# Half-row matmuls of a mixer block issued as alternating pairs, with new settings of the kernel's own scheduler

## The chip, the core and the metric

The kernel runs on one core of a Trainium2 chip. The metric is the device time of one execution in microseconds (us), lower is better. All times here are of this one core; "the profile" is one profiled execution of the kernel before, with its trace.

## What is computed

A causal decoder trunk of two layers over 256 tokens of width 1024, all in fp32. Cut to what matters here:

```python
for l in range(DEPTH):                                   # 2 layers
    h = modulate(rms_norm(x, norm_mix[l]), sh1, sc1)
    p = h @ w_in[l]                                      # one wide projection
    q, k = apply_rope(...), apply_rope(...)              # 8 heads of 64
    y_att  = dilated_mixture_attention(q, k, v)          # scores q.k over a head's 64 channels
    y_rwkv = rwkv7_time_mix(p[..., i0:i1], ...)          # decay: tanh(xw) @ w_up, rate: xa @ a_up, inner width 64
    y_gmlp = chunked_spatial_gating(p[..., i1:i2], ...)
    merged = sum(sigmoid(gate_i) * (y_i @ w_branch[l][i]))
    x = x + gt1 * (merged @ w_out[l])
    h = modulate(rms_norm(x, norm_ffn[l]), sh2, sc2)
    x = x + gt2 * conv_gated_ffn(h, w_up, conv, w_down)
return rms_norm(x, norm_final)
```

## The kernel before

**The main stream.** The weights arrive as a stream of chunks of 128x2048, two halves of 128x1024 each. A half is loaded by DMA into a `raw` buffer, rounded to the fast fp32r format (`whi`, a cast on ScalarE or VectorE, line 458 or 459), and the rest is formed on VectorE (`wlo = raw - whi`, line 462). The activations are split in the same way (`hhi`, `hlo`), and a product is three fp32r matmuls into one PSUM bank: high by high, high by low, low by high. These matmuls are called main matmuls here. They are chained in a fixed order (the `main` flag of `pe()`), layer by layer: the mixers' projections, then the gated MLP.

**The side work.** Between the main matmuls stand small matmuls in plain fp32, which TensorE runs as two passes each, and which the trace shows as two MATMUL records: the RWKV recurrence in two halves of four heads (`rwkv_half`), attention (`attention`), the chunked gating (`gmlp`) and the normalisations. A matmul whose contraction is 64 long uses half of the PE rows. There are two kinds: the decay and rate products of `rwkv_half` (`lora` weights, operands `th` in partitions 0 to 63 and `xa` in 64 to 127), and the attention scores (`m01` holds q and k; a pair of heads lies in partitions 0 to 63 and 64 to 127). In the profile the scores read `bka<-m`, the decay and rate products `bkr<-zx,lora`. Matmuls with 64 output columns use half of the PE columns; those are written in alternating order already (`gmlp`, `turned`).

**Names that the text uses.** Banks of PSUM are `bkm` (three, main), `bkr` (three, RWKV) and `bka` (two, attention, gating and norms). `head_rsqrt` sums squares by the matmul `bkr<-cst,tt`, adjusts on VectorE (`rs`, line 482), takes a power on GpSimd (line 709), spreads it on ScalarE or VectorE into `gt`, and turns that on TensorE (`bkr<-vec,gt`); the output norm of a half goes through `rs` in the same way and is turned by `bkr<-vec,kkn`. A small triangular system goes through DRAM (`scb`) and comes back by DMA into `Tc`, from which VectorE makes `sig`, which TensorE turns (`bkr<-vec,sig`).

**What sets the order.** Every operation is recorded with an engine (or two to choose from), an assumed cost and its dependences (`Plan.add`, `Plan.either`). `Plan.flush` then makes an order for all engines before anything is emitted: `forward` places operations by priority on a model of the engines, `backward` makes new priorities from the ends, `ROUNDS` times, and the order with the lowest modelled end is emitted. So every assumed cost and setting can move every instruction. `pe()` assumes 0.035 us for the second of two neighbouring matmuls that use different halves of the columns; `rsqrt` assumes 0.5 us on GpSimd; `DMA_ISSUE`, `DMA_BW` describe the loads.

Of the kernel before, what the change touches and what calls it, by code (L numbers as in the profile page):

```python
# [3 lines left out]

# [7 lines left out]
F32 = mybir.dt.float32  # L12
# [52 lines left out]
    "A01 W00 W01 A00 A10 A20 W10 W11 A21 A11 W20 A31 A30 A40 W21 A41 "  # L65
    "A60 A51 A50 W30 W31 A61 W40 A71 W41 W50 W51 A70"
).split()]
ROUNDS = 12
BOOST = {'ahead': 30, 'norm': 100, 'rstd': 3}
MAIN = False  # L70
ADA_ENG = ['DVE DVE DVE DVE DVE DVE DVE DVE'.split(), 'DVE PE PE DVE PE DVE PE DVE'.split()]
# [14 lines left out]
class Plan:  # L86
# [8 lines left out]
           ("PE", "DVE"): 0.2, ("POOL", "ACT"): 0.075, ("POOL", "DVE"): 0.075, ("POOL", "PE"): 0.15,  # L95
           ("ACT", "ACT"): 0.0, ("PE", "PE"): 0.0, ("POOL", "POOL"): 0.06, ("SP", "SP"): 2.0}
    DMA_LAT = 0.95
    DMA_ISSUE = 1.1
    DMA_BW = 360e3

    def __init__(self, nc):
        self.nc = nc
# [100 lines left out]
    def forward(self, prio):  # L203

        ops = self.ops
        free, avail, wait, self.ticks = {}, {}, {}, {}
        for e in ("ACT", "DVE", "PE", "POOL", "SP"):
            free[e], avail[e], wait[e] = 0.0, [], []
        for o in ops:
            o.left, o.done, o.ready = len(o.deps), False, [0.0] * len(o.alts)  # L210

        def push(o):
            for n, a in enumerate(o.alts):
                heapq.heappush(wait[a[0]], (o.ready[n], o.i, n, o))

        for o in ops:
            if not o.left:
                push(o)
        order = []
        table, dma = 0, 0.0  # L220
        todo = len(ops)
        while todo:
            best = None
            for e in free:
                t, w, a = free[e], wait[e], avail[e]
                while w and (w[0][3].done or w[0][0] <= t):
                    x = heapq.heappop(w)
                    if not x[3].done:
                        heapq.heappush(a, (prio[x[1]], x[1], x[2], x[3]))
                while a and a[0][3].done:  # L230
                    heapq.heappop(a)
                if a:
                    st = t
                elif w:
                    st = w[0][0]
                else:
                    continue
                if best is None or st < best[0]:
                    best = (st, e)
            st, e = best  # L240
            w, a = wait[e], avail[e]
            while w and w[0][0] <= st:
                x = heapq.heappop(w)
                if not x[3].done:
                    heapq.heappush(a, (prio[x[1]], x[1], x[2], x[3]))
            _, _, n, o = heapq.heappop(a)
            if o.done:
                continue
            cost = o.alts[n][1]
            if len(o.alts) > 1:  # L250
                f, c, _ = o.alts[1 - n]
                at = max(free[f], st) + sum(x[3].alts[x[2]][1] for x in avail[f] if not x[3].done and x[0] < prio[o.i])
                if max(at, o.ready[1 - n]) + c < st + cost + (self.KEEN if e == "DVE" else -self.KEEN):
                    t = max(at + c - cost, st + 0.05)
                    heapq.heappush(w, (t, o.i, n, o))
                    if not any(x[3] is o for x in avail[f]) and not any(x[3] is o for x in wait[f]):
                        heapq.heappush(wait[f], (o.ready[1 - n], o.i, 1 - n, o))
                    continue
            o.done = True
            todo -= 1  # L260
            o.on = n
            if e == "SP":
                free[e] = st + 0.5
                dma = o.end = max(dma, st + self.DMA_ISSUE) + cost
            elif e == "PE":
                free[e] = o.end = self.stream(st, cost, o.work)
            else:
                if e == "ACT" and o.table and o.table != table:
                    st, table = st + 1.28, o.table
                free[e] = o.end = st + cost  # L270
            order.append(o)
            for s, raw in o.succ:
                for m, b in enumerate(s.alts):
                    r = o.end + self.lat(e, b[0], raw)
                    if r > s.ready[m]:
                        s.ready[m] = r
                s.left -= 1
                if not s.left:
                    push(s)
        return max(max(free.values()), dma), order, [o.on for o in ops]  # L280
# [51 lines left out]
    def flush(self):  # L332
# [6 lines left out]
        for o in reversed(ops):  # L339
# [1 line left out]
            for s, raw in o.succ:  # L341
                m = max(m, s.cp + self.lat(o.eng, s.eng, raw) * o.w)
            o.cp = m + (o.cost + (self.DMA_ISSUE if o.eng == "SP" else 0.0)) * o.w + o.b
        best = None
        prio = [-o.cp for o in ops]
        self.log = []
        for k in range(ROUNDS):
            r = self.forward(prio)
            self.log.append(r[0])
            ends = [o.end for o in ops]  # L350
            if best is None or r[0] < best[0]:
                best, top = r, ends
            if k == ROUNDS - 2:
                for o, n in zip(ops, best[2]):
                    o.on = n
                ends = top
            prio = [-t for t in self.backward([-e for e in ends])]
        for o, n in zip(ops, best[2]):
            o.on = n
# [22 lines left out]
def decoder(ctx: ExitStack, tc: tile.TileContext, xT, crow_d, cst_d, vec_d, wada, stream, small, lnrow, bsrow, out):  # L382
# [28 lines left out]
    def pe(mms, main=False):  # L411
        cost, work, outs, ins, half = 0.0, 0.0, [], [], None
        for m in mms:
            o, a, b = m[0], m[1], m[2]
            outs.append(o)
            ins += [a, b]
            was, half = half, (o.ap[0][1] == 64 and divmod(o.offset, o.ap[0][0])[0] or 0, o.ap[0][1] == 64)
            if was is not None and was[1] and half[1] and was[0] != half[0]:
                cost, half = cost + 0.035, None
                continue  # L420
            work += _n(b) / 2400 * (1 if len(m) == 3 or a.dtype == F32R else 4)
            if len(m) == 3:
                cost += 0.112
            elif a.dtype == F32R:
                cost += max(_n(b) / 2400 + 0.0112, 0.112)
            else:
                cost += 2 * max(_n(b) / 1200 + 0.003, 0.1115)

        def emit():
            for m in mms:  # L430
# [179 lines left out]
    def load():  # L610
# [5 lines left out]
        for h in range(2):  # L616
# [1 line left out]
            dma(src, stream[i][:, h * 1024:(h + 1) * 1024], after=hold[0] if i in (START, START + 1) else None)  # L618
            hi, lo = ring("whi", whis), ring("wlo", wlos)
            acopy(hi, src)  # L620
            sub(lo, src, hi.bitcast(F32))
            halves.append((hi, lo))
        loaded.append(halves)

# [81 lines left out]


    def rsqrt(xc, y, t):
        P.add("POOL", 0.5, lambda: nc.gpsimd.tensor_tensor(y, xc, minus_half.to_broadcast(list(xc.shape)), op=OP.pow),  # L709
              [y], [xc, minus_half])  # L710

    def cols(w):
# [86 lines left out]
    def rwkv_half(l, hf, W, lora, th, xa, sg, yhi, ylo):  # L799
# [41 lines left out]

        yield f"k{hf}"
        take(f"k{hf}")
        pw = bank()
        pe([(bnc(pw, i), lora[0:64, (n0 + i) * 128:(n0 + i + 1) * 128], th[0:64, :], True, True) for i in range(2)])
        for i in range(2):
            act(sig[:, i, :], bnc(pw, i), AF.Tanh, scale=0.5, bias=dv[:, l, 14 + n0 + i:15 + n0 + i])
        ts(sig, sig, 0.5, 0.5, OP.mult, OP.add)
        pa = bank()
        pe([(bnc(pa, i), lora[64:128, (n0 + i) * 128:(n0 + i + 1) * 128], xa[64:128, :], True, True)  # L850
            for i in range(2)])
        for i in range(2):
            act(aa[:, i, :], bnc(pa, i), AF.Tanh, scale=0.5, bias=dv[:, l, 18 + n0 + i:19 + n0 + i])
        ts(aa, aa, 0.5, 0.5, OP.mult, OP.add)
# [218 lines left out]
    def attention(l, W, yhi, ylo):  # L1073
# [20 lines left out]
        s2 = W["s2"] + [W["m3"][:, i * 512:(i + 1) * 512] for i in range(2)]  # L1094
        for n in range(4):
            T2 = []
            for hs in H:
                ps = bank("at")
                pe([(ps[:, 0:128], q[hs, n, 0:128], k[hs, n, 0:128], True, True),
                    (ps[:, 128:384], q[hs, n, 128:256], k[hs, n, :], True, True)])  # L1100
                p = ring("s2", s2)[:, 0:384]
                st = ring("ast", W["ast"])
                stt(p, ps[:, 0:384], 0.125, ab, OP.mult, OP.add)
# [444 lines left out]
```

## Time and profile before

| | |
|---|---|
| time, median of 3 runs | 1061.46 us (1059.19 to 1063.53) |
| profiled execution, own time | 1065.56 us |
| its span, first to last instruction | 1063.8 us |
| mean granted TensorE clock | 0.981 |
| TensorE matmul busy | 1008.1 us (95%) |
| VectorE busy | 896.0 us (84%) |
| ScalarE busy | 526.9 us (50%) |
| GpSimd busy | 34.4 us (3%) |

In rows of the trace, PE is TensorE, DVE VectorE, ACT ScalarE, POOL GpSimd and SP the engine that issues the DMAs. A row of a timeline has start, length, engine, line, operation, output and inputs, and in brackets how long the engine sat idle before it and what ended that. A row of the waits has the total, the number of times and the longest. A row of a table by stretches has the stretch, its length, the busy time of each engine and its instructions, the granted clock (PEclk, 1.00 is full), and the DMA share. [...]

### The profile page before, as it was taken

How to read it: one execution, taken by the hardware profiler on the slowest of the kernel's cores; microseconds unless marked ns; L12 is line 12 of the kernel's file. 1: busy time of each engine (PE TensorE's matmuls, PEld its weight loads, DVE VectorE, ACT ScalarE, POOL GpSimd, SP SyncE). 2: the span in 40 equal slices, each digit the busy share in tenths (PEclk: the TensorE clock that was granted, in tenths of full speed). 3: DMA queues.
4: the chain of work that ended last, by engine and by line, in shares of the span. 5: the costliest groups of instructions: out<-in, count | busy, mean ns of one | idle time of the engine just before them, and what ended most of it. 6: DMA issues, size and time to landing. Idle time of an engine off the chain costs nothing. (4 is left out here: it accounts for less than half of the span.)

```text
span 1063.8 us, 20460 instructions
## 1 busy us (share of the span) xinstructions
PE 1008.1 (95%) x8042; PEld 968.8 (91%) x8042; DVE 896.0 (84%) x1820; ACT 526.9 (50%) x917; POOL 34.4 (3%) x27
## 2 busy tenths in 40 slices
PE   5999998899999999999999999889999999999996
PEld 4989997689889999999999899879899999999996
DVE  6979999889769899999999799679976789877753
ACT  4364456656434555544436645455643465343341
POOL 0010000100000000000010100010000000000000
PEclk9999999899999899999999999999999999999998
DMA  9888565364578668988995454415434646555541
GB/s 350 322 279 264 190 210 185 118 203 162 186 257 275 201 218 299 315 287 279 380 314 191 146 163 138 157 34 182 134 118 136 217 143 207 190 181 187 185 143 40
DMA packets 70130, 217.65 MB, mean 205 GB/s; under 512 B 15121, under 2 KB 17169, under 8 KB 69522
## 3 DMA queue, kind: packets, MB, share of 16 engines
q1 hardware_dynamic: 70034, 216.35, 60.8%
q8 instruction: 63, 1.03, 0.4%
q14 instruction: 33, 0.27, 0.1%
HBM read 212.12 MB, written 4.19 MB: 203 GB/s over the span
## 5 line engine op out<-in xcount | busy, mean ns | idle before, releaser
L434 PE MATMUL bkm<-hhi,whi 128*128 128x256 f32 x1104 | 322.0, 292 | 5.2 <-DVE m L462 4.0
L462 DVE TENSOR_TENSOR wlo<-raw,whi 128x1024 fp32r<-128x1024 f32 x235 | 285.7, 1220 | 43.5 <-ACT whi L458 42.5
L434 PE MATMUL bkm<-hlo,whi 128*128 128x256 f32 x1104 | 314.5, 285 | 1.6 <-DVE hlo L495 1.6
L434 PE MATMUL bkm<-hhi,wlo 128*128 128x256 f32 x1104 | 314.0, 284 | 0.0
L458 ACT CAST whi<-raw 128x1024 fp32r<-128x1024 f32 x198 | 206.8, 1047 | 214.8 <-PE bkm L434 105.8
L434 PEld LDWEIGHTS bkm<-hhi,whi 128*128 128x128 f32 x1104 | 213.3, 193 | 11.8 <-issue 10.3
L434 PEld LDWEIGHTS bkm<-hlo,whi 128*128 128x128 f32 x1104 | 213.6, 193 | 2.4 <-DVE hlo L495 2.0
L434 PEld LDWEIGHTS bkm<-hhi,wlo 128*128 128x128 f32 x1104 | 213.4, 193 | 0.0
L434 PE MATMUL bkr<-hhi,whi 128*128 128x256 f32 x368 | 104.5, 284 | 0.0
L434 PE MATMUL bkr<-hlo,whi 128*128 128x256 f32 x368 | 104.5, 284 | 0.0
L434 PE MATMUL bkr<-hhi,wlo 128*128 128x256 f32 x368 | 104.4, 284 | 0.0
L434 PEld LDWEIGHTS bkr<-hhi,whi 128*128 128x128 f32 x368 | 71.1, 193 | 0.0
L434 PEld LDWEIGHTS bkr<-hlo,whi 128*128 128x128 f32 x368 | 71.0, 193 | 0.0
L434 PEld LDWEIGHTS bkr<-hhi,wlo 128*128 128x128 f32 x368 | 71.0, 193 | 0.0
L495 DVE SCALAR_TENSOR_TENSOR bd<-bd,crow 128x1024 f32<-128x1024 f32 x52 | 63.3, 1220 | 5.2 <-DMA bd<-in_wada_dram 5.0
L462 DVE TENSOR_TENSOR wlo<-m,whi 128x1024 fp32r<-128x1024 f32 x45 | 54.9, 1220 | 14.0 <-ACT whi L458 13.8
L458 ACT CAST whi<-m 128x1024 fp32r<-128x1024 f32 x39 | 40.8, 1047 | 49.2 <-PE bkm L434 23.3
L709 POOL TENSOR_TENSOR rs<-rs,vec 128x8 f32<-128x8 f32 (+2 forms) x17 | 23.4, 1377 | 766.8 <-DVE rs L482 668.6
L434 PE MATMUL bkm<-ygh,whi 128*128 128x256 f32 (+1 forms) x156 | 46.4, 298 | 0.6 <-ACT ygh L458 0.4
L434 PE MATMUL bkm<-ygl,whi 128*128 128x256 f32 x156 | 44.6, 286 | 1.7 <-DVE ygl L462 1.6
L434 PE MATMUL bkm<-ygh,wlo 128*128 128x256 f32 (+1 forms) x156 | 44.2, 284 | 0.0
L495 DVE SCALAR_TENSOR_TENSOR raw<-raw,crow 128x1024 f32<-128x1024 f32 x34 | 41.2, 1218 | 3.6 <-DMA raw<-in_wada_dram 3.6
(520 smaller groups left out, 2203.4 us busy)
## 6 DMA issues: line engine op xcount, KB each, us to landing
raw<-in_stream_dram SPq DMA_DIRECT2D x238, 512.0 KB, 4.7
bd<-in_wada_dram SPq DMA_DIRECT2D x52, 512.0 KB, 5.9
m<-in_stream_dram SPq DMA_DIRECT2D x47, 512.0 KB, 4.8
raw<-in_wada_dram SPq DMA_DIRECT2D x34, 512.0 KB, 5.1
m<-in_wada_dram SPq DMA_DIRECT2D x7, 512.0 KB, 8.7
scx<-x SPq DMA_DIRECT2D x2, 1024.0 KB, 10.0
x<-scx SPq DMA_DIRECT2D x2, 1024.0 KB, 7.0
x<-in_xT_dram SPq DMA_DIRECT2D x4, 256.0 KB, 4.2
```

The source lines that it names most:

```text
L434: nc.tensor.matmul(m[0], m[1], m[2], start=m[3], stop=m[4], skip_group_check=len(m) > 5)
L458: P.either([("ACT", _act(a), lambda: nc.scalar.copy(o, a)), ("DVE", 0.07 + _n(a) / (960 if _psum(o, a) else 1920), lambda: nc.vector.tenso ...
L462: P.add("DVE", 0.07 + _n(a) / 960, lambda: nc.vector.tensor_tensor(o, a, b, op=op), [o], [a, b])
L495: P.add("DVE", c, lambda: nc.vector.scalar_tensor_tensor(o, a, s, b, op0=op0, op1=op1, **k), [o, accum], ins)
L709: P.add("POOL", 0.5, lambda: nc.gpsimd.tensor_tensor(y, xc, minus_half.to_broadcast(list(xc.shape)), op=OP.pow), [y], [xc, minus_half])
```

## The change

Four things change.

1. `rwkv_half` issues the decay and the rate products as one group of four, alternating between the row halves, into two banks. `attention` issues the scores of a pair of heads as one group of four, alternating between the heads, into both `bka` banks.
2. `pe()` now assumes the low cost for the second of two neighbours also where they use different halves of the rows, and some of its other costs change.
3. The scheduler: 100 rounds in place of 12, with random changes to the ends from round 9 on; VectorE may be held idle for up to 0.15 us for a more urgent operation; assumed DMA latency and bandwidth and the GpSimd power's cost change.
4. For the chunks below number 35 (layer 0's mixers and the first ones behind them) `wlo` is formed in two instructions of 512 columns in place of one of 1024.

```diff
-ROUNDS = 12
+ROUNDS, SEED = 100, 1
+FINE = 35
+HOLD, SHORT, WAIT, URGENT = ("DVE",), 0.5, 0.15, 10.0
...
-    DMA_ISSUE = 1.1
-    DMA_BW = 360e3
+    DMA_ISSUE = 1.75
+    DMA_BW = 340e3
...
+            if e in HOLD and cost > SHORT:
+                near = [x for x in w if not x[3].done and x[0] <= st + WAIT and prio[x[1]] < prio[o.i] - URGENT]
+                if near:
+                    heapq.heappush(a, (prio[o.i], o.i, n, o))
+                    free[e] = min(x[0] for x in near)
+                    continue
...
-                free[e] = st + 0.5
+                free[e] = st + 0.4
...
-            if k == ROUNDS - 2:
+            if k > 8:
                 for o, n in zip(ops, best[2]):
                     o.on = n
-                ends = top
+                s = (0.3, 1.0, 1.0, 3.0)[k % 4]
+                ends = [e + rng.gauss(0.0, s) for e in top]
...
-            was, half = half, (o.ap[0][1] == 64 and divmod(o.offset, o.ap[0][0])[0] or 0, o.ap[0][1] == 64)
-            if was is not None and was[1] and half[1] and was[0] != half[0]:
+            was, half = half, [(y.ap[0][1] == 64, divmod(y.offset, y.ap[0][0])[0]) for y in (o, a)]
+            if was is not None and any(p[0] and q[0] and p[1] != q[1] for p, q in zip(was, half)):
                 cost, half = cost + 0.035, None
...
-                cost += max(_n(b) / 2400 + 0.0112, 0.112)
+                cost += max(_n(b) / 2400 + 0.0125, 0.112)
...
-                cost += 2 * max(_n(b) / 1200 + 0.003, 0.1115)
+                cost += 2 * max(_n(b) / 1200 + 0.003, 0.1115) + (0.097 if a.ap[0][1] == 64 and _n(b) > 128 else 0.0)
...
-            sub(lo, src, hi.bitcast(F32))
+            for q in (slice(0, 512), slice(512, 1024)) if i < FINE else (slice(0, 1024),):
+                sub(lo[:, q], src[:, q], hi[:, q].bitcast(F32))
...
-        P.add("POOL", 0.5, lambda: nc.gpsimd.tensor_tensor(...), [y], [xc, minus_half])
+        P.add("POOL", {1: 0.6, 2: 1.65, 8: 2.65}[_n(xc)], lambda: nc.gpsimd.tensor_tensor(...), [y], [xc, minus_half])
...
-        pw = bank()
-        pe([(bnc(pw, i), lora[0:64, (n0 + i) * 128:(n0 + i + 1) * 128], th[0:64, :], True, True) for i in range(2)])
+        pw, pa = bank(), bank()
+        pe([(bnc(p, i), lora[h, (n0 + i) * 128:(n0 + i + 1) * 128], r[h, :], True, True)
+            for i in range(2) for p, h, r in ((pw, H[0], th), (pa, H[1], xa))])
...
-        pa = bank()
-        pe([(bnc(pa, i), lora[64:128, (n0 + i) * 128:(n0 + i + 1) * 128], xa[64:128, :], True, True)
-            for i in range(2)])
...
-            for hs in H:
-                ps = bank("at")
-                pe([(ps[:, 0:128], q[hs, n, 0:128], k[hs, n, 0:128], True, True),
-                    (ps[:, 128:384], q[hs, n, 128:256], k[hs, n, :], True, True)])
+            pss = [bank("at") for _ in H]
+            pe([x for c, kc in ((0, 128), (128, 256)) for ps, hs in zip(pss, H)
+                for x in [(ps[:, c:c + kc], q[hs, n, c:c + 128], k[hs, n, 0:kc], True, True)]])
+            for ps in pss:
```

The built programs have the same 7468 instructions on PE. VectorE goes from 1730 to 1800, ScalarE from 879 to 869. Three places show what moves.

First, TensorE in layer 0 at the start of the second RWKV half, before. `zx,lora` is the decay product, `cst,tt` the sum of squares of `head_rsqrt`, `vec,gt` the turn at its end.

```order
L434 MATMUL bka_100<-m_115 128x128
L434 MATMUL bka_100<-m_115 128x256
L432 MATMUL bkr_96<-vec,kkn_156 128x128 x4
L434 MATMUL bkr_98<-zx_158,lora 128x256 x2
L434 MATMUL bkr_96<-cst,tt_157 128x2 x4
L432 MATMUL bkr_97<-vec,gt_155 128x128 x4
L434 MATMUL bkm_95<-whi_81,hhi 128x512
```

The same place now; the left-out rows are main matmuls.

```order
L442 MATMUL bkr_96<-vec,kkn_156 128x128 x4
L444 MATMUL bkr_97<-zx_158,lora 128x256
L444 MATMUL bkr_98<-zx_158,lora 128x256
L444 MATMUL bkr_97<-zx_158,lora 128x256
L444 MATMUL bkr_98<-zx_158,lora 128x256
L444 MATMUL bkr_96<-cst,tt_157 128x2 x4
L444 MATMUL bkm_95<-hhi,whi_80 128x256
...
L442 MATMUL bka_99<-vec,m_0_138 128x128 x3
L442 MATMUL bka_100<-vec,s_1_160 128x128 x3
L442 MATMUL bkr_97<-vec,gt_155 128x128 x4
L444 MATMUL bkm_95<-whi_81,hhi 128x512
```

The decay and rate products alternate between the banks 97 and 98, and between the sum of squares and the turn of `gt` there are now 24 main matmuls and six turns of attention, where nothing stood before.

Second, TensorE at the first attention scores of layer 0, before:

```order
L434 MATMUL bkm_94<-hhi,wlo_84 128x256
L434 MATMUL bka_99<-m_115 128x128
L434 MATMUL bka_99<-m_115 128x256
L434 MATMUL bkm_94<-hhi,whi_81 128x256
L434 MATMUL bkm_94<-hlo,whi_81 128x256
```

And now:

```order
L444 MATMUL bkr_98<-bdS,zr_150 64x128
L444 MATMUL bka_99<-m_115 128x128
L444 MATMUL bka_100<-m_115 128x128
L444 MATMUL bka_99<-m_115 128x256
L444 MATMUL bka_100<-m_115 128x256
L444 MATMUL bkr_97<-bd_1_147,bd_1_146 128x128
```

Two heads stand in one group, alternating between the two banks, where one head stood alone between main matmuls; the other head came 41 rows later.

Third, VectorE early in layer 0's mixers, before, where `wlo` is one instruction:

```order
L459 CAST whi_81<-raw_77 128x1024
L462 TENSOR_TENSOR wlo_85<-raw_77,whi_81 128x1024
L462 TENSOR_TENSOR m_115<-m_115,cst 128x1024
L482 TENSOR_SCALAR rs_91<-bkr_98 128x8
L482 TENSOR_SCALAR sig_152<-sig_152 128x512
```

And now:

```order
L469 COPY gt_155<-rs_91 128x512
L472 TENSOR_TENSOR wlo_85<-raw_77,whi_81 128x512
L492 TENSOR_SCALAR sig_152<-sig_152 128x512
L472 TENSOR_TENSOR wlo_85<-raw_77,whi_81 128x512
L492 TENSOR_SCALAR aa_153<-aa_153 128x512
```

An instruction of the RWKV chain stands between the halves of `wlo`. 116 instructions of this half size take the place of 58.

More of the change, by code (lines that the diff above doesn't have):

```diff
@@ L2 @@
 import math
+import random
 from contextlib import ExitStack
@@ L343, in flush @@
             o.cp = m + (o.cost + (self.DMA_ISSUE if o.eng == "SP" else 0.0)) * o.w + o.b
-        best = None
+        best, rng = None, random.Random(SEED)
         prio = [-o.cp for o in ops]
@@ L708, in rsqrt @@
     def rsqrt(xc, y, t):
-        P.add("POOL", 0.5, lambda: nc.gpsimd.tensor_tensor(y, xc, minus_half.to_broadcast(list(xc.shape)), op=OP.pow),
+        P.add("POOL", {1: 0.6, 2: 1.65, 8: 2.65}[_n(xc)], lambda: nc.gpsimd.tensor_tensor(y, xc, minus_half.to_broadcast(list(xc.shape)), op=OP.pow),
               [y], [xc, minus_half])
```

## The prediction

> **What bounds the kernel now.** I read the page first, then the busy time of each engine in the four large stretches, then who TensorE waited for, then the granted clock behind the waits, and last the timeline at the matmuls that change. The page:
>
> ```profile
> span 1063.8 us, 20460 instructions
> PE 1008.1 (95%) x8042; PEld 968.8 (91%) x8042; DVE 896.0 (84%) x1820; ACT 526.9 (50%) x917; POOL 34.4 (3%) x27
> ```
>
> The stretches are layer 0's mixers, layer 1's mixers, layer 0's gated MLP and layer 1's:
>
> ```profile
> 60.00:350.00 290.00, 269.00 (x2110) 251.27 (x2109) 251.54 (x552) 151.87 (x279) 11.54 (x8) 0.97 0.64 209
> 552.00:842.00 290.00, 277.30 (x2191) 259.12 (x2190) 239.31 (x517) 153.51 (x283) 12.93 (x9) 0.99 0.46 149
> 350.00:552.00 202.00, 199.85 (x1639) 199.65 (x1638) 196.65 (x376) 102.65 (x162) 3.44 (x2) 0.97 0.83 284
> 842.00:1054.00 212.00, 211.75 (x1776) 211.75 (x1777) 157.59 (x262) 91.29 (x145) 0.70 (x1) 1.00 0.51 167
> ```
>
> TensorE is the bound everywhere. In the MLPs it is idle for 2.4 us in 414 and nothing there changes, so whatever the change does is done in the mixers: there TensorE is idle for 21.0 + 12.7 = 33.7 us in 580. Beside it VectorE stands at 87% in layer 0's mixers and 83% in layer 1's. A mixer's time is therefore TensorE's work, plus its waits for short chains on other engines. The largest waits of layer 0's mixers, and then of layer 1's:
>
> ```profile
> PE bkr L432 <- ACT gt L458: 6.0, 2, 4.0
> PE bkm L434 <- DVE m L462: 4.0, 1, 4.0
> PE bkr L432 <- DVE sig L462: 2.0, 1, 2.0
> PE bkr L432 <- DVE kkn L462: 1.9, 2, 1.7
> ```
>
> ```profile
> PE bkr L432 <- DVE sig L462: 2.3, 1, 2.3
> PE bkr L432 <- ACT gt L458: 1.9, 1, 1.9
> ```
>
> A wait has a second price. Behind the long ones the granted clock is halved:
>
> ```profile
> 166.90:170.30 3.40, 3.40 (x17) 3.40 (x18) 3.15 (x11) 1.09 (x4) 0.00 (x0) 0.50 0.50 144
> 201.10:211.30 10.20, 6.31 (x16) 4.85 (x17) 8.21 (x19) 5.24 (x12) 2.49 (x1) 0.50 0.32 103
> 283.00:286.40 3.40, 3.40 (x24) 2.85 (x24) 2.60 (x5) 2.31 (x4) 0.00 (x0) 0.50 0.80 261
> 678.90:682.30 3.40, 3.40 (x25) 2.96 (x23) 2.36 (x4) 2.00 (x4) 0.00 (x0) 0.50 0.43 135
> ```
>
> These four stretches follow the waits for `m` (4.0), for the second `gt` (4.0) and the two for `sig` (2.0 and 2.3). At half clock about half of TensorE's busy time is lost: 1.7 us in each of the three short ones, 6.31 / 2 = 3.2 us in the long one.
>
> **The pairs.** A score group of one head, a decay group, and the starts of the main matmuls behind them:
>
> ```profile
> 175.43 0.92 PE L434 MATMUL bka<-m 64*128 64x128 f32 x4
> 176.28 0.39 PE L434 MATMUL bkm<-hhi,whi 128*128 128x256 f32 x1
> ...
> 193.69 1.02 PE L434 MATMUL bkr<-zx,lora 64*128 64x256 f32 x4
> 194.65 0.39 PE L434 MATMUL bkm<-hhi,whi 128*128 128x256 f32 x1
> ...
> 598.05 1.13 PE L434 MATMUL bkr<-zx,lora 64*128 64x256 f32 x4
> 599.11 0.39 PE L434 MATMUL bkm<-hhi,whi 128*128 128x256 f32 x1
> ```
>
> Start to next start, a score group holds TensorE for 0.85 us and a decay or rate group for 1.06. There are 16 score groups (2 layers, 8 heads) and 8 of the other kind (2 layers, 2 halves, decay and rate). If the two members of a pair run wholly side by side, a pair costs what one costs: 8 x 0.85 + 4 x 1.06 = 11.0 us are saved.
>
> If they run one behind the other, only the entry into half-row work is saved, 12 times. The group at 193.69 stood behind another half-row group and took 0.96 in place of 1.06, so an entry is 0.10 and the saving 1.2 us. Below that lies a loss: were 0.10 due at each change of the half, as at an entry, 12 groups of 8 passes would pay up to 12 x 7 x 0.10 = 8.4 us. I take no loss, because the nearest rows are the pairs that alternate between halves of the columns, against full-width ones of the same number of passes:
>
> ```profile
> 79.71 1.95 PE L434 MATMUL bkr<-BK,bd 128*128 128x128 f32 x16
> 81.41 0.48 PE L434 MATMUL bkm<-whi,hhi 128*128 128x512 f32 x1
> ...
> 99.43 1.09 PE L434 MATMUL bka<-m,m 128*64 128x128 f32 x16
> 100.45 0.39 PE L434 MATMUL bkm<-hhi,whi 128*128 128x256 f32 x1
> ```
>
> Sixteen full-width passes take 1.70 us, sixteen alternating half-column passes 1.02. Two halves of the array do run at once here, and alternating costs nothing visible. No row shows it for halves of the rows. I take 11.0 and keep 1.2 as the other end.
>
> A row speaks about weights:
>
> ```profile
> L434 PEld LDWEIGHTS bkr<-zx,lora x48: 182/187/193, 65.6 to 767.2; 64*128 64x128 f32 x32, 128*128 128x128 f32 x16
> ```
>
> Loading weights of 64 rows takes no less than 128 rows, 182 to 193 ns for both, and a half-row pass still loads 128 columns, where a half-column pass loads 64. So the column pairs do not prove that two such loads go side by side. [...]
>
> **The order: waits for the power on GpSimd.** The chain of one wait for `gt`:
>
> ```profile
> 199.73 1.02 PE L434 MATMUL bkr<-cst,tt 128*128 128x2 f32 x8 [0.62 <-ACT Dx L452]
> ...
> 201.24 0.16 DVE L482 TENSOR_SCALAR rs<-bkr 128x8 f32<-128x8 f32 x1
> ...
> 201.54 2.49 POOL L709 TENSOR_TENSOR rs<-rs,vec 128x8 f32<-128x8 f32 x1 [4.92 <-DVE rs L482]
> ...
> 204.06 0.62 ACT L458 COPY gt<-rs 128x512 f32<-128x512 f32 x1 [1.71 <-POOL rs L709]
> ...
> 204.73 1.12 PE L432 MATMUL bkr<-vec,gt 128*128 128x128 f32 x4 [3.97 <-ACT gt L458]
> ```
>
> The order before was made with 0.5 us for the power; the trace has 2.49. So TensorE was sent into the wait with nothing to do. The new order was made with 2.65 and puts 24 main matmuls and six turns there. In layer 1's MLP 1776 instructions, nearly all of them main matmuls, take 211.75 us, 0.12 each. So 24 give 2.9 us, and the six turns (12 passes at 1.70 / 16) 1.3 us: 4.2 against the wait of 4.0. The wait goes, and with it the 3.2 us of half clock behind it. What could be late next there is the bank `bkm` of those main matmuls, whose readers are not in this chain.
>
> The other waits for `gt`: by the order of instructions layer 0's first half has 24 main matmuls at that place and had 9, wider ones among both; some 1.5 of its 2.0 us go. Layer 1's second half has 48 where it had 18, 3.6 us more against 1.9. Together 4.0 + 1.5 + 1.9 = 7.4, and 3.2 of clock. The last turn of a half (`kkn`, 1.7 of the 1.9) has 48 main matmuls in front where it had 36, 1.4 us: I count 1.4.
>
> **The order: the rest.** The waits for `sig` hang on DMA, and the assumed DMA latency goes up from 1.1 to 1.75; that for `m` hangs on nothing that the change corrects. Those are 4.0 + 4.3 us and 3 x 1.7 = 5.1 of clock. I take half, 6.7, between nothing and 13.4.
>
> On the other side, an order that is drawn anew has waits of its own. The named waits are 7.9 + 4.0 + 4.3 + 1.7 = 17.9 of the 33.7 us of idle time; 15.8 stay unnamed. Then there is `wlo` in halves:
>
> ```profile
> L462 DVE TENSOR_TENSOR wlo<-raw,whi 128x1024 fp32r<-128x1024 f32 x235 | 285.7, 1220 | 43.5 <-ACT whi L458 42.5
> ...
> L462 DVE TENSOR_TENSOR sq<-sq,cst 128x512 f32<-128x512 f32 x8 | 5.5, 684 | 0.5 <-ACT sq L458 0.5
> ```
>
> Two of 684 against 1220 ns are 0.148 us more, 58 times 8.6 us of VectorE; TensorE's work hides it as long as VectorE is idle for 290 - 251.5 = 38.5 us in layer 0's mixers. For both together I charge 12 us, most of the unnamed waits once more; the ends are 0 and 25. The hold of VectorE is at most 0.15 us at a time and is counted in this charge. The DMA order at the start changes in a few rows, and TensorE's first wait there is for a small load that stays early: nothing.
>
> **The sum.** 11.0 + 7.4 + 3.2 + 1.4 + 6.7 - 12 = 17.7 us. The profiled execution's own time is 1065.56, its span 1063.8; so it becomes 1047.9. The median of the runs shown is 4.1 us below that execution, and I take the forecast there: 1043.8, say 1044.
>
> **The rivals.** *Row halves do not overlap.* For: loads as long as for full rows, no row pair in the trace. Against: the column pairs. Then 1.2 in place of 11.0: 1054. *The waits are nearly all filled.* The same sum without half of the charge and with all of the rest's 13.4 us: 12.7 us better, 1031. *Nothing comes of it:* TensorE gets through its work sooner, but the end of a mixer is set by the chain of VectorE, ScalarE and DMA, so that saved work turns into waits and the redrawn order wins only what it loses. For: VectorE's 87%. Against: TensorE worked through 580 us with 33.7 idle. That gives 1061 less a few: 1058 to 1062.
>
> *Slower: VectorE becomes the bound of layer 0's mixers.* 8.6 us come from the halves, 12 further instructions move to it from ScalarE and elsewhere (1800 - 1730 - 58), at 0.5 us some 6, and if 40 of its long operations are held for 0.15, another 6: 21 us. It decides from the point at which the 38.5 us of idle time cannot be used, since they are themselves waits for ScalarE and DMA. Then layer 0's share of the pairs, 5.5, is lost, the waits move instead of going, and 21 - 5.5 = 15 are added: 1077.
>
> **How the numbers follow.** Forecast 0.60, row halves without overlap 0.12, nearly all filled 0.12, nothing 0.10, VectorE 0.06. The forecast's own ends, from the charge's ends of 0 and 25, are 1032 and 1057. To leave out no more than 2 in 10 the range goes from 1030, just past the better rival, to 1058, the near edge of "nothing". About 0.5%, 5.3 us, is what a measurement of this kernel can tell from no change, so faster means below 1056.2: 0.60 and 0.12 whole, and most of 0.12, 0.81. Same has most of "nothing" and what is left of the others, 0.12; slower 0.07.
>
> **What would show it right or wrong.** In the profile after: the records of a row pair start some 10 ns apart, and the groups of eight passes hold TensorE for about 0.85 and 1.06 us, where 1.6 and 2.0 would mean no overlap. The waits for `gt` are below 1 us in total, and no stretch of half clock follows the second one. TensorE's idle time in the mixers is about 20 us in place of 33.7. VectorE stays under 95% in layer 0's mixers. The prediction is wrong if the idle time is not lower, if new waits of 2 us and more stand in the mixers with half clock behind them, or if TensorE's chain ends late in the MLPs, which I take as unchanged.

## The result and the profile after

The changed kernel takes 1028.33 us (median of 4 runs, 1026.11 to 1029.76) where the kernel before took 1061.83 beside it: a ratio of 0.9685 with a 95% interval of 0.9658 to 0.9712, 33.5 us less. The forecast was 1044, some 17.5 less. The direction and most of the places were right, the size was not: the time lies 1.7 us below the low end of the range. The profiled execution took 1029.76 us, with a span 35.8 us shorter than before.

The page of the changed kernel:

```profile
span 1028.0 us, 20481 instructions
...
PE 990.1 (96%) x8042; PEld 952.3 (93%) x8042; DVE 895.2 (87%) x1890; ACT 529.0 (51%) x907; POOL 33.4 (3%) x27
```

The four large stretches, cut at the same main matmuls as before (where the order at a cut changed, to within 1 us): layer 0's mixers, layer 1's mixers, layer 0's MLP, layer 1's MLP.

```profile
58.90:335.60 276.70, 263.23 (x2111) 245.53 (x2110) 252.61 (x612) 157.92 (x286) 8.36 (x6) 0.99 0.67 222
532.10:806.20 274.10, 268.87 (x2192) 253.07 (x2190) 239.67 (x524) 158.81 (x286) 14.38 (x9) 1.00 0.50 165
335.60:532.10 196.50, 196.14 (x1638) 195.26 (x1637) 194.61 (x380) 93.81 (x142) 2.51 (x2) 1.00 0.81 278
806.20:1017.10 210.90, 210.62 (x1766) 210.63 (x1767) 156.58 (x259) 91.84 (x146) 0.70 (x1) 1.00 0.52 168
```

Layer 0's mixers are 13.3 us shorter, layer 1's 15.9, and layer 0's MLP, which the prediction held unchanged, 5.5. TensorE's idle time in the mixers is 13.5 + 5.2 = 18.7 us where it was 33.7. Its waits over the whole span (total, times, longest):

```profile
PE bkm L444 <- DMA m<-in_crow_dram: 4.5, 1, 4.5
PE bkr L442 <- DVE sig L472: 4.1, 3, 1.9
PE bka L444 <- DMA VK<-in_wada_dram: 3.7, 1, 3.7
PE bkm L444 <- DVE wlo L472: 3.0, 5, 1.3
...
PE bka L442 <- POOL rs L720: 2.2, 2, 1.1
PE bkr L442 <- ACT gt L468: 1.4, 1, 1.4
```

The two from DMA stand at the start, ahead of the mixers. In the mixers `gt` has fallen from 7.9 to 1.4, and the wait of 4.0 for `m` before a main matmul is gone, while `sig` has hardly moved (4.3 to 4.1). Row pairs and the chain of the second wait for `gt`, from the timeline:

```profile
172.49 0.93 PE L444 MATMUL bka<-m 64*128 64x128 f32 x8
173.34 0.49 PE L444 MATMUL bkr<-bd,bd 128*128 128x128 f32 x2
...
187.22 1.13 PE L444 MATMUL bkr<-zx,lora 64*128 64x256 f32 x8
188.38 1.02 PE L444 MATMUL bkr<-cst,tt 128*128 128x2 f32 x8
...
194.40 0.66 PE L442 MATMUL bkr<-vec,gt 128*128 128x128 f32 x4 [1.36 <-ACT gt L468]
...
223.84 1.33 PE L444 MATMUL bka<-m 64*128 64x128 f32 x8
225.10 0.38 PE L444 MATMUL bkm<-hhi,whi 128*128 128x256 f32 x1
```

In six of the eight score groups two heads' scores, 8 records where there were 4, hold TensorE for the 0.85 us that one head's 4 held it before, and the two members start 6 ns apart in the raw records. In the other two, at 223.84 and 737.69, the members overlap only in part, and the groups take 1.26 and 1.46 us; why is not shown. Groups are timed from start to next start, since records overlap: a main matmul's lasts 0.28 us and the next one starts 0.12 us after it (191.27 and 191.39). So timed, idle time left out, all groups together took 22.0 us before and take 12.2 now.

The clock: before the end of the program one stretch is left at half clock, behind a wait of 1.88 us for `sig`. Before, there were six, 34.0 us together: the four of the prediction (20.4), one of 3.4 at the start of layer 1's mixers, and one of 10.2 in layer 0's MLP, behind a wait of 2.15 us at 352.4. After, then before:

```profile
152.60:156.00 3.40, 3.40 (x24) 2.84 (x23) 2.67 (x6) 2.85 (x4) 0.00 (x0) 0.51 0.63 227
```

```profile
354.70:364.90 10.20, 10.20 (x48) 10.20 (x49) 8.52 (x15) 4.55 (x7) 1.62 (x1) 0.50 0.72 242
```

In the second row TensorE is busy throughout, so a view of idle time shows nothing, and yet a main matmul takes 0.21 us there where it takes 0.12 at full clock. TensorE was busy for 30.1 of the 34.0 us; half of that, an estimate from the granted clock of 0.50, makes about 15 us lost before, 1.7 now.

### The profile page after: what moved, and what is told of

Same layout as the page of the kernel before. It is cut to its first block, busy times and chain, and to the rows that moved or that the text cites. A ratio compares the mean times of both kernels' runs of the same rounds, so it can differ in the third digit from the quotient of the medians.

```text
span 1028.0 us, 20481 instructions
## 1 busy us (share of the span) xinstructions
PE 990.1 (96%) x8042; PEld 952.3 (93%) x8042; DVE 895.2 (87%) x1890; ACT 529.0 (51%) x907; POOL 33.4 (3%) x27
## 5 line engine op out<-in xcount | busy, mean ns | idle before, releaser
L468 ACT CAST whi<-raw 128x1024 fp32r<-128x1024 f32 x208 | 217.8, 1048 | 228.4 <-PE bkm L444 112.1
L472 DVE TENSOR_TENSOR wlo<-raw,whi 128x1024 fp32r<-128x1024 f32 (+1 forms) x293 | 293.4, 1008 | 42.3 <-ACT whi L468 41.5
L468 ACT CAST whi<-m 128x1024 fp32r<-128x1024 f32 x37 | 38.8, 1048 | 49.4 <-PE bkr L444 18.9
```

The costliest lines, as they stand in the source:

```text
L468: P.either([("ACT", _act(a), lambda: nc.scalar.copy(o, a)), ("DVE", 0.07 + _n(a) / (960 if _psum(o, a) else 1920), lambda: nc.vector.tenso ...
L472: P.add("DVE", 0.07 + _n(a) / 960, lambda: nc.vector.tensor_tensor(o, a, b, op=op), [o], [a, b])
```

## The experiments

The theory after the result had three parts, in this order: the pairs overlap because their members alternate; the filled waits for `gt` and the clock behind them are worth tens of us; and the order became dense because the assumed durations were corrected, GpSimd's above all. The rivals: being neighbours is enough for the pairs; a wait taken away returns elsewhere; and it was the long search, or luck in its draw, that found the order. Eighteen kernels were run, in five groups, each group beside its own runs of the kernel before (medians 1061.4 to 1063.2). Where "seed" is said, the new search ran with another start of its random numbers.

### The pairs

**One half behind the other**, the rest of the order untouched:

```diff
-            for m in mms:
+            for m in mms if turn is None else [mms[i] for i in turn]:
...
-  (decay and rate, scores)  pe([...])
+  (decay and rate, scores)  pe([...], turn=(0, 2, 1, 3))
```

> The order of all engines as in the changed kernel; only inside the 12 groups the two halves of the rows are issued one behind the other (0, 2, 1, 3) in place of alternating. Theory 1 (the pairs run side by side and TensorE is the bound, so their saving shows in full): the groups go from about 0.86 and 1.06 us to 1.6 and 1.9, 8 x 0.75 + 4 x 0.86 = 9.4 us, and the time goes up by 8 to 11 us, to 1036 to 1039. Rival (the saved work of TensorE turns into waits): up by less than 3 us.

Measured: 1027.66 us, ratio 0.9671 [0.9639, 0.9703], the same as the changed kernel. The first score group of this kernel:

```profile
170.99 0.93 PE L444 MATMUL bka<-m 64*128 64x128 f32 x8
171.85 0.49 PE L444 MATMUL bkr<-bd,bd 128*128 128x128 f32 x2
```

0.86 us again, though bank 99 is now served twice before bank 100 is. The trace puts the records of the two halves 13 ns apart. All groups together take 12.6 us where they take 12.2 alternating. Here two halves that stood next to each other in the queue ran side by side; the alternation added nothing that the time shows (1028.33 with it). My expectation of 8 to 11 us was wrong.

**A matmul on all rows, ahead of each pair or between its halves.** Both kernels do the same extra work, a one-column product into a bank that the next matmul overwrites:

```diff
+                run = [mms[i] for i in turn]
+                run.insert(0, (full, ident, one, True, True))    # ahead
+                run.insert(2, (full, ident, one, True, True))    # between
```

> The changed kernel's order, the halves issued one behind the other, and in each of the 12 groups one added full-row matmul (128x1, two passes) ahead of the group, whose output is written over. It separates nothing. Theory 1 (two row halves run side by side wherever they stand next to each other in TensorE's queue): groups stay at about 0.86 and 1.06 us, plus about 0.3 us each for the added matmul, so 1030 to 1033. Rival as in the next run.

> The same instructions as the run with the added matmul ahead of the group, but it stands between the two halves. Theory 1: it parts the halves, a group takes about 0.8 us more than with the added matmul ahead, 12 groups 9 to 10 us, and the time is 7 to 12 us over that run, at 1038 to 1043. Rival (the overlap is not worth its TensorE time, since saved work turns into waits): within 3 us of that run.

Measured: 1026.84 us (0.967 [0.9619, 0.9722]) ahead, 1038.87 (0.977 [0.9731, 0.9809]) between: 12.0 us apart. One score group with it ahead, then with it between:

```profile
169.49 0.38 PE L448 MATMUL bka<-vec 128*128 128x1 f32 x2
169.80 0.93 PE L448 MATMUL bka<-m 64*128 64x128 f32 x8
170.66 0.49 PE L448 MATMUL bkr<-bd,bd 128*128 128x128 f32 x2
```

```profile
172.06 0.92 PE L448 MATMUL bka<-m 64*128 64x128 f32 x4
172.91 0.38 PE L448 MATMUL bka<-vec 128*128 128x1 f32 x2
173.22 0.92 PE L448 MATMUL bka<-m 64*128 64x128 f32 x4
174.07 0.49 PE L448 MATMUL bkr<-bd,bd 128*128 128x128 f32 x2
```

1.17 us against 2.01; in the decay and rate groups 1.28 against 2.43 (539.27 to 540.55, and 546.17 to 548.60). 8 x 0.84 + 4 x 1.15 = 11.3 us; all twelve added up, idle time left out, 14.3 against 25.8, 11.5. This is what the overlap saves of TensorE's time in an order that is otherwise the same, and the forecast's 11.0 was right as such. The 12.0 us of the kernels' times are not as clean a measure. With the matmul ahead nothing is left at half clock before the end of the program; with it between, two stretches are, 10.2 us together, behind a decay and rate group each, though TensorE waits for nothing there:

```profile
190.10:193.50 3.40, 3.40 (x17) 3.40 (x17) 2.71 (x6) 0.87 (x3) 1.72 (x1) 0.50 0.15 46
667.90:674.80 6.90, 6.90 (x34) 6.90 (x35) 4.22 (x8) 2.95 (x4) 1.96 (x1) 0.51 0.23 76
```

By half of TensorE's 10.3 us of busy time some 5 us are lost in them, so that 11.5 + 5 stand against 15.3 between the spans of the two profiled executions (1022.5 and 1037.8) and 12.0 between the medians: that 12.0 is near 11.0 is in part luck. And the twelve added matmuls, 0.31 us each, cost nothing that the time shows when they stand ahead (1026.84 against 1027.66 without them, where 1030 to 1033 was expected), so TensorE's time did not go into the kernel's one for one here.

**Pairs alone, in the old settings**, and **the new settings without pairs**, both with an order drawn anew:

```diff
 (before)   the decay, rate and score matmuls of the change, and how a pair is counted
 (after)    the decay, rate and score matmuls as they were
```

> The kernel before with the pairs and the assumed cost of the second half alone; costs and search as before. Theory 1: 8 to 13 us faster than before, 1049 to 1054. Rival (orders drawn with wrong costs differ by their waits more than by the pairs): not within 5 us of that, 1044 or less or 1059 or more.

> The changed kernel with the decay, rate and score matmuls issued as before, head by head, and drawn anew with the new settings; with the seeds so far orders of the same settings differ by some 6 us. Theory 1 (overlap is worth 9 to 12 us in a kernel that TensorE bounds): 1034 to 1047. Rival (the pairs only pay through the one order on record): 1033 or less.

Measured: 1059.75 us (0.9973 [0.9949, 0.9997]) and 1042.93 (0.9818 [0.9785, 0.9851]). The mixers of the pairs alone, cut at the main matmuls at which they were cut before:

```profile
60.70:349.20 288.50, 264.99 (x2099) 247.19 (x2098) 248.32 (x553) 154.74 (x281) 10.91 (x7) 0.97 0.64 210
548.10:837.30 289.20, 274.61 (x2187) 258.50 (x2187) 236.84 (x520) 150.43 (x276) 12.15 (x9) 0.98 0.45 145
```

They are 2.3 us shorter than before (290.0 each), with 23.5 + 14.6 = 38.1 us idle in place of 33.7, and there are again 34 us of half clock. This is the outcome of the rival "nothing comes of it": TensorE did less and waited more. In the change as a whole the waits went as well. Without pairs the new settings give 1042.93 in their one draw, 7 to 15 us above the three draws with pairs below.

### The waits for the power

**Only the cover taken away**: what TensorE does between the sum of squares and the turn of `gt`, and the turn does not need, is put off until behind the turn, in the finished order of the changed kernel. In three of the four halves nothing stays between them; in layer 0's first half 12 of 24 main matmuls do.

```diff
+    def bare(self, order, first, last):
+        (what `last` needs, found through deps)
+        return self.shift(order, [o for o in order[i + 1:j] if o.eng == "PE" and o not in need], last)
...
-        for o in best[1]:
+        for o in seq:
```

> The changed kernel, with the main matmuls that stand between the sum of squares and the turn of gt put off until behind the turn, in all four RWKV halves as far as dependences allow; nothing else is drawn anew. Theory 2 (a long wait of TensorE costs itself and a stretch of half clock behind it): the waits for gt go from 1.4 us to 9 to 12 us, stretches of half clock of 3.4 or 10.2 us stand behind those of 2 us and more, and the time goes up by 13 to 25 us, to 1041 to 1053. Rival (what was put off fills later waits): the waits for gt come back, but others shrink, no half clock, up by less than 6 us.

Measured: 1052.40 us, 0.9903 [0.9865, 0.994], 24.1 us above the changed kernel. Its waits at these four places (lines are 25 further down), and the granted clock of two of the four stretches at half clock:

```profile
PE bkr L467 <- ACT gt L493: 9.1, 2, 5.0
...
PE bkr L467 <- DVE gt L494: 4.4, 1, 4.4
...
PE bkr L467 <- ACT sig L487: 2.6, 1, 2.6
```

```profile
70.12:76.95 6.83, 4.90 (x15) 3.86 (x14) 5.09 (x11) 0.84 (x2) 0.00 (x0) 0.50 0.67 203
196.41:203.24 6.83, 4.31 (x20) 4.32 (x21) 2.42 (x4) 1.67 (x3) 0.20 (x1) 0.50 0.45 154
```

The four waits are 16.1 us in place of 1.4, and at each stands 6.8 us of half clock, which begins within the three longer waits (at 196.4, say, in the one from 193.9 to 198.9) and just behind the shortest. TensorE was busy for 18.7 us in these four stretches, so by half 9.3 are lost, while the changed kernel's own stretch of half clock, 1.7 us lost, is gone: 14.7 + 9.3 - 1.7 = 22.3 of the 24.1. A wait of 4 us cost about 6 here, an estimate from the 16.1 us of waits and the 9.3 lost with them. The cover is worth that in this order; it is not what the change brings there, since before only 7.9 us were waited for `gt`.

### Which setting found the order

**All assumed durations as before**, with the first seed and with a second one:

```diff
-    DMA_ISSUE = 1.75
-    DMA_BW = 340e3
+    DMA_ISSUE = 1.1
+    DMA_BW = 360e3
...
-        P.add("POOL", {1: 0.6, 2: 1.65, 8: 2.65}[_n(xc)], ...
+        P.add("POOL", 0.5, ...
     (and SP's 0.5 and the two matmul costs)
```

> The changed kernel with all assumed costs of before (GpSimd's power 0.5, DMA latency 1.1 and bandwidth 360e3, issue 0.5, the two matmul costs), the order drawn with 100 rounds as now. Theory 3 (true costs fill the waits): the waits for gt are 6 us or more, two or more stretches of half clock come back, up by 10 to 20 us, to 1038 to 1048. Rival (the longer search brings the gain): up by less than 5 us.

> All assumed costs of before with the long search as in the earlier run, another seed. Theory 3: 1043 to 1060 again. Rival (the earlier run was a bad draw): 1038 or less.

Measured: 1052.76 (0.9885 [0.9836, 0.9934]) and 1045.78 (0.984 [0.9804, 0.9875]). But the waits for `gt`, which were to be 6 us or more, are 2.5 us in the first: the time is lost in other places.

**The new settings with other seeds**, to see what a draw is worth:

```diff
-ROUNDS, SEED = 100, 1
+ROUNDS, SEED = 100, 2
```

> The changed kernel with another seed of the random changes, so another order from the same settings. If the settings give the gain: 1022 to 1036. Rival (the order on record is a lucky draw): 1040 or more.

> The changed kernel with a third seed. If the settings give the gain: 1024 to 1038. Rival (lucky draw): 1040 or more.

Measured: 1034.81 (0.9727 [0.9686, 0.9768]) and 1036.22 (0.9752 [0.972, 0.9783]). With the changed kernel's 1028.33 the new settings spread over 8 us and the old durations over 7, and the two do not touch: 1028 to 1036 against 1046 to 1053. The durations matter. The spread is also the limit of everything below: a single kernel that differs by less than some 8 us from the three shows nothing of its setting.

**The old search** (12 rounds, nothing random) with the new durations:

```diff
-ROUNDS, SEED = 100, 1
+ROUNDS, SEED = 12, 1
-            if k > 8:
+            if k == ROUNDS - 2:
-                ends = [e + rng.gauss(0.0, s) for e in top]
+                ends = top
```

> The changed kernel with the search of before, 12 rounds without random changes, and the new costs. Theory 3: waits for gt stay under 2 us, up by 2 to 8 us, to 1030 to 1036. Rival (the longer search brings the gain): up by 12 us or more.

Measured: 1048.41 us, 0.9865 [0.9832, 0.9897], 20 us above the changed kernel and 12 above the slowest of the seeds. Its idle time in the mixers is 28.8 us and its half clock 23.9. So the search matters too, as far as one order tells.

**Single durations put back**: GpSimd's, DMA's, the two matmul costs.

```diff
-        P.add("POOL", {1: 0.6, 2: 1.65, 8: 2.65}[_n(xc)], ...      (GpSimd)
+        P.add("POOL", 0.5, ...
-    DMA_ISSUE = 1.75                                               (DMA)
-    DMA_BW = 340e3
+    DMA_ISSUE = 1.1
+    DMA_BW = 360e3
     (and SP's 0.4 back to 0.5)
-   max(_n(b) / 2400 + 0.0125, 0.112), ... + (0.097 if ... else 0.0)   (matmul)
+   max(_n(b) / 2400 + 0.0112, 0.112), ...
```

> The changed kernel with the assumed cost of GpSimd's power alone put back to 0.5. Theory 3 (true costs fill the waits): waits for gt, kkn and rs together 4 us or more over those of the changed kernel (4.5 with the two of the norms), 1036 to 1050. Rival (this cost is not what matters): 1022 to 1035.

> The changed kernel with the assumed DMA latency and bandwidth of before alone, drawn anew. All old costs together gave 1046 and 1053 with two seeds, new ones 1028, 1035 and 1036 with three. If the DMA costs are what matters: waits for sig (a DMA's result) 5 us or more in place of 4.1, and 1040 to 1053. Rival (they do not matter): 1026 to 1038.

> The changed kernel with the two assumed matmul costs of before alone (a main matmul 1.3 ns shorter, no surcharge on half-row ones), drawn anew. If TensorE's pace in the plan is what matters, since 1.3 ns times some 3000 main matmuls up to the end of layer 1's mixers is a drift of 4 us against all other engines: 1038 to 1053. Rival: 1026 to 1038.

Measured: GpSimd 1029.03 (0.9685 [0.9657, 0.9714]), DMA 1047.79 (0.9867 [0.9844, 0.9889]), matmul 1033.20 (0.9735 [0.9697, 0.9774]). With GpSimd's price put back to 0.5 us, TensorE's longest waits and those at the turns of `gt` are (one of them is put down to `ACT sig`):

```profile
PE bkm L444 <- DMA m<-in_crow_dram: 5.8, 1, 5.8
PE bka L442 <- POOL rs L720: 5.1, 4, 2.2
...
PE bkr L442 <- ACT sig L462: 1.2, 1, 1.2
...
PE bkr L442 <- ACT gt L468: 0.7, 1, 0.7
PE bkr L442 <- DVE gt L469: 0.7, 1, 0.7
```

The order still has 24 main matmuls at the second `gt`, and 0.7 us of waiting there. So the corrected price is not needed to fill that wait; that part of the theory, and the prediction's reason, falls. The price is not without effect: the turns of `gt` wait for 3.3 us in all in place of 1.4, the norms behind `rs` for 5.1 in place of 2.2, but the time does not show it. DMA's assumption is the one that matters alone, by 12 to 19.5 us against the three seeds. Of the orders with pairs and the long search, the three with DMA's old assumption (alone once, with all the others twice) lie at 1046 to 1053, and the seven with the corrected one and VectorE's hold (three seeds, GpSimd's price, the matmul costs, and two more below) at 1028 to 1036. What it changes shows in VectorE's waits for DMA, with the old assumption and then in the changed kernel:

```profile
DVE raw L505 <- DMA raw<-in_wada_dram: 6.8, 4, 2.5
DVE bd L505 <- DMA bd<-in_wada_dram: 5.5, 3, 2.6
DVE cs L472 <- DMA top<-sca: 3.5, 3, 1.6
DVE whi L469 <- DMA raw<-in_stream_dram: 3.3, 2, 2.2
DVE x L505 <- DMA x<-scx: 1.0, 1, 1.0
```

```profile
DVE whi L469 <- DMA raw<-in_stream_dram: 2.4, 4, 1.1
DVE cs L472 <- DMA top<-sca: 2.1, 2, 1.5
DVE bd L505 <- DMA bd<-in_wada_dram: 1.7, 1, 1.7
DVE sig L472 <- DMA Tc<-scb: 1.5, 1, 1.5
DVE x L505 <- DMA x<-scx: 1.5, 2, 0.9
DVE raw L505 <- DMA raw<-in_wada_dram: 1.0, 3, 0.5
```

20.1 us against 10.2. TensorE is idle for 50.4 us of the span against 37.9, and half clock is 20.5 us against 3.4. That the one leads to the other is not shown: the second and third seeds have 17.4 and 16.7 us of such waits on VectorE and are still at 1035 and 1036, while the old search has 10.3 at 1048 and the kernel without the hold (below) 8.3 at 1041.5. Longer waits for `sig`, which were expected, are not the way either, since they are 3.6 us there.

**DMA from both sides.** If the correction matters because it comes nearer to the truth, more of it should be no worse; and alone, in the kernel before, it should bring something. The page gives 4.6 us from issue to landing of a streamed load in the changed kernel:

```profile
raw<-in_stream_dram SPq DMA_DIRECT2D x238, 512.0 KB, 4.6
```

The old assumption comes to 1.1 + 512 KB / 360e3 + 0.95 = 3.5 us, the new one to 4.2, and one of 2.2 to 4.7.

```diff
-    DMA_ISSUE = 1.75         (changed kernel)
+    DMA_ISSUE = 2.2
-    DMA_ISSUE = 1.1          (kernel before)
-    DMA_BW = 360e3
+    DMA_ISSUE = 1.75
+    DMA_BW = 340e3
```

> The changed kernel with an assumed DMA latency of 2.2, so that a 512 KB load is planned to be there after 2.2 + 1.54 + 0.95 = 4.7 us, which is what the trace shows (4.6 to 4.8), where 1.75 plans 4.2 and 1.1 with the old bandwidth 3.5. If the nearness of the plan's loads to the real ones is what carries the costs' part: 1022 to 1036, no worse than the three seeds, and VectorE's waits for DMA at 16 us or less. Rival (1.75 only fits the order on record): 1038 or more.

> The kernel before with the new assumed DMA latency and bandwidth alone, search of 12 rounds, no pairs. If this one correction carries the costs' part by itself: 1042 to 1052. If it pays only with the long search: 1056 to 1066.

Measured: 1033.22 (0.9723 [0.9677, 0.9769]), within the spread of the seeds, with 9.2 us of VectorE's waits for DMA; and 1052.69 (0.9915 [0.9878, 0.9953]), 8.7 us faster than before, with VectorE's waits for DMA down from 26.7 to 11.4. So the correction works in the old kernel too, for about half of what it is worth beside the long search, each from one order.

**Hold and halves.** VectorE without the hold, and `wlo` whole:

```diff
-HOLD, SHORT, WAIT, URGENT = ("DVE",), 0.5, 0.15, 10.0
+HOLD, SHORT, WAIT, URGENT = (), 0.5, 0.15, 10.0
...
-FINE = 35
+FINE = 0
```

> The changed kernel without holding VectorE for a more urgent operation, drawn anew. If the hold matters: 1037 or more in both layers' mixers. Rival: 1026 to 1037, as the seeds differ.

> The changed kernel with wlo in one instruction of 1024 throughout, drawn anew. If the halves help (a chain's instruction waits at most half as long behind a wlo): 1034 to 1045, and layer 0's mixers, where they stand, lose more than layer 1's. Rival (they are the cost that was charged): 1022 to 1028.

Measured: 1041.50 (0.9804 [0.9782, 0.9825]) and 1035.38 (0.9751 [0.9725, 0.9778]). The second lies among the seeds, and layer 0's mixers, where most of the halves are, take 275.6 us in it and 276.0 in the changed kernel: no effect of the halves is shown either way. The first is 5 us above the slowest seed, which suggests that the hold helps; one draw does not settle it.

## Why the prediction was wrong in size, by its own steps

**The pairs: right.** 11.0 forecast, 11.5 in the groups of the two kernels made for it, and 9.8 (22.0 - 12.2) in the changed kernel, where two groups overlap only in part. A score pair that overlaps in full takes 0.86 us, alternating or in series, where one head took 0.85, and 2.01 once a matmul on all rows stands between the halves (1.17 with it ahead). That two such loads go side by side, which the column pairs left unproved, shows in the trace: in the changed kernel's score group at 172.49 the records of a pair's first two loads, 182 and 183 ns long, start 7 ns apart.

**The named waits: right in size, for a partly wrong reason.** `gt` fell by 6.5 (forecast 7.4), `kkn` from 1.9 to 0.9 (forecast 1.4 less), `m` by 4.0 and `sig` by 0.2 (forecast 4.2 for both). What is left of `gt` is 1.4 us, not below 1, and it is the second wait, which the prediction took as gone whole. And most of `gt` is filled with GpSimd's old price too.

**The charge: the step that failed.** "For both together I charge 12 us, most of the unnamed waits once more." It set the redrawn order's own waits nearly as high as all the waits that were to go, so the sum let idle time fall by 1.0 us, while the text beside it expected "about 20 us in place of 33.7". Measured: 18.7. The two statements contradict each other, and the second was right. In the terms of the sum: the unnamed waits of the mixers were 15.8 us and were to become 27.8; without `gt`, `kkn` and `sig` (6.5 us) they are 12.2 now. So the term, 12 us of loss, was a gain of some 3.6. The halves of `wlo` do cost VectorE what was forecast, 0.685 us twice where 1.220 stood once, but TensorE waited for `wlo` 3.0 us in all (before, none shows). The rows:

```profile
L472 DVE TENSOR_TENSOR wlo<-raw,whi 128x1024 fp32r<-128x1024 f32 x177 | 215.5, 1220 | 36.3 <-ACT whi L468 35.7
...
L472 DVE TENSOR_TENSOR wlo<-raw,whi 128x512 fp32r<-128x512 f32 x116 | 78.0, 685 | 6.0 <-ACT whi L468 5.9
```

The charge had been set by the old order's unnamed waits, as if an order could only be shuffled. The long search and DMA's correction made it better: without the one or the other the kernel takes 20 us longer, 12 longer than the slowest seed, and TensorE is idle in the mixers for 28.8 us (old search) and 30 (old assumption). In the second and third seed it is idle there for 22.4 and 22.8 us, so that the charge was too high in each of the three draws.

**The clock: under-counted.** 3.2 and half of 5.1 were forecast, 5.8 us; 13.3 went. "In the MLPs TensorE is idle for 2.4 us in 414 and nothing there changes" overlooked the 10.2 us at half clock in layer 0's MLP, because only idle time was read there. It also left the 3.4 us at the start of layer 1's mixers out. The page's clock line before the change, in slices of 26.6 us, has its second dip in the fourteenth, 346 to 372 us, which is that MLP:

```profile
PEclk9999999899999899999999999999999999999998
```

**The sizes together**, from the forecast's -17.7 to the span's -35.8: idle time in the mixers 14.0 more than forecast, the clock 7.6, idle time in layer 0's MLP 1.8, ahead of the mixers and at the end 1.0, which makes 24.4. The pairs are 1.2 less, and about 5 us went the other way: TensorE's records are busy for that much longer than pairs and clock explain (1008.1 - 990.1 = 18.0, where 9.8 + 13.3 = 23.1 were due). Some 1.7 of them are the rounding of the clock's price to a half: a main matmul takes 0.21 us at half clock (355.93 to 356.14, before) where it takes 0.12 at full (351.88 to 352.00). What the rest is stays open.

**The rivals.** "The waits are nearly all filled", at 1031, came nearest by its time, but 18.7 us of waits are left and `sig` stayed. VectorE did not become the bound: it is busy for 91% of layer 0's mixers (252.61 of 276.70). "Nothing comes of it" is what the pairs alone did.

**What stays open.** The kernel that was timed is the fastest of three draws of its settings; the other two, 1034.8 and 1036.2, lie within the forecast's range. So some 7 us of the miss can be put down to the draw, which is luck, and I cannot say what in that order is lucky. The hold, the halves and how the durations other than DMA's add up cannot be told apart at 8 us of spread. The old search and DMA's old assumption alone were drawn once each. No kernel here is faster than the changed one beyond its uncertainty (1026.84 and 1027.66 are the lowest).

## What to carry to other kernels

When a change redraws an instruction order, cost its new waits by what the search now knows, with several seeds, and not by the waits of the old order; then check that the idle time in your sum is the idle time you say you expect. Read the granted clock everywhere, also where TensorE is never idle, since 10.2 us of half clock stood behind a wait of 2.15 us in the kernel before, and another 10.2 came without a wait in the one with a full matmul between the halves. And before you credit one corrected number, put back that number alone: here the one with the best story, GpSimd's, showed no effect on the time, and DMA's was worth 12 to 19.5 us.

## What the runs showed of the hardware

**Neighbours ran together.** In these kernels matmuls on different halves of the rows ran together where they stood next to each other: their records lie 13 ns apart in series and 6 ns alternating, with the same 0.86 us for a score group. One matmul on all rows between them ended it, at 0.84 us more for a score group (2.01 against 1.17) and 1.15 for a decay and rate group (2.43 against 1.28). Not every pair overlapped in full: two of the twelve groups of the changed kernel did so only in part, at 1.26 and 1.46 us.

**Half clock came in steps of 3.4 us** ahead of the end of the program: 3.4 or 10.2 us long in the kernel before, 3.4 in the changed one, 6.8 with the cover taken away, and once 13.7 (the kernel before with DMA's correction, at 202.8). It did not go by the length of the wait alone. In the kernel with the second seed 10.2 us of it began within a wait of 1.46 us at 549.5:

```profile
550.00:560.20 10.20, 7.98 (x36) 7.69 (x37) 8.63 (x17) 5.14 (x8) 4.96 (x1) 0.50 0.46 149
```

In the kernel before, 10.2 us of it began 0.3 us into a wait of 3.97, one of 4.03 was followed by 3.4 and one of 2.0 (at 71.0) by none. The 10.2 us of the kernel with the full matmul between the halves had no wait ahead of them at all, and TensorE was busy for 3.40 of 3.40 and 6.90 of 6.90 us in their two stretches. What sets off half clock is not settled here.
